# Changing the order of the filler work, and joining small steps, in a two-group hybrid encoder layer

## The chip, the cores and the metric

The kernel runs on one core of a Trainium2 chip. The metric is device time in microseconds (us) of one execution. The engines are named as in the profile: PE (matrix multiplications, with its weight loads as PEld), DVE, ACT and POOL (elementwise work), and SP, whose queue issues nearly all DMAs.

## The reference

One layer is applied to a prompt of 512 tokens and a sample of 1024 tokens, 1024 features each. Four mixers work on parts of one input projection, and their outputs, gated, go through one output projection:

```python
h = rms_norm(x, pre_g) * (1 + scale[:, None, :]) + shift[:, None, :]
proj = h @ w_in
a_q, a_k, a_v, a_lr, b_u, c_q, c_k, c_v, d_u, d_v, z = jnp.split(proj, splits, axis=-1)
out_a = gla_branch(a_q, a_k, a_v, a_lr, ...)      # chunked gated linear attention, both directions
out_b = fnet_branch(b_u, fnet_w)                  # Fourier transform over tokens and channels
out_c = attention_branch(c_q, c_k, c_v, ...)      # 8 query heads, 2 key heads, rms norm and rotary (rope)
out_d = sgu_branch(d_u, d_v, ...)                 # gating: w_s mixes 128 tokens, times d_u
mixed = jnp.concatenate([out_a, out_b, out_c, out_d], axis=-1) * jax.nn.silu(z)
y = rms_norm(mixed @ w_out, post_g)
return x + gate[:, None, :] * y
```

`scale`, `shift` and `gate` come from `silu(c) @ ada_w + ada_b`, one vector for the prompt and one for the sample.

## The kernel before

Everything is float32. Each operand of a large product is split in a high and a low part, and a product is made of three matmuls (high by high, high by low, low by high). The tokens are three groups of 512: group 2 is the prompt, groups 0 and 1 are the halves of the sample.

There are two streams of work. The **foreground** is a chain: GLA's first pass of a group (`gla_in`, six `level` steps, states), GLA's second pass (`gla_pass2`), FNet, the layout of keys and values (`kv_path`), and attention (`attend`). The **filler** is the projections, written under `later()`, which gives them a lower priority: `a_start` and `a_path` (GLA's q, k, v and low-rank gate), `zpath` (ten jobs, each evacuated by ACT and by one DVE product `zr`), `sgu` (two projections and the mixing product, tiles `dvu` and `vhl`), `b_path` (FNet's input), `c_kv` and `c_q` (keys and queries, with rope: tiles `kev`, `cev`, `rp_t`, `ropess`), and `out_ops`, `out_first`, `out_last` (the operand of the output projection, built per block of 128 features from a tile `mt` of the mixers' output and a tile `zt`, and the projection's column groups, `j` = 0 to 3). Small tables in DRAM (`zT`, `mixd`, `qd`, `kvd` and the like) carry results from filler to foreground and back.

The next group's operand is prepared in three steps: `in_prep_x(g)` loads the rows of x (`xt`), squares and sums them on ACT (`jk`, `xss`) and makes a scaled identity `rsb` on DVE; `in_prep_b` spreads it with one matmul of `ones` and `rsb`; `in_prep_t` loads x transposed (`xT`, stored under the tile `ze`), scales it on DVE (`h`, in the tile `zr`) and splits it into `oph` and `opl`. `gate_path` makes half of the output gate.

A scheduler at build time merges both streams into one fixed order per engine, by priority and modelled times; at run time each engine issues in that order, and an instruction that waits holds all behind it. A matmul level of GLA is tied to the filler: `LEVEL_AT` gives, per group, the thousands of filler columns after which the first level may be issued, and the step between levels. Filler products go to two PSUM buffers (`ps_mm`), scores and levels to three (`ps_s`), transposes to three, so a filler job can wait for the evacuation of the job before the last. Buffers in SBUF under one tag are shared: `xy` (two) by `xt`, `dvu`, `vhl` and `yt`; `ze` and `zr` (three each) by z, `xT`, `mt` and `zt`.

The filler's order is: group 2: a, z, sgu, b, then `queries(2, 0)`, which is in_prep_x(0), c_kv(2), in_prep_b, c_q(2) with in_prep_t(0), gate; group 0: a, z, sgu, b, then `queries(0, 1)`; group 1: b, a, z, sgu, c_kv. Beside the second pass and attention stand c_q(1), then the output projection of groups 2, 0 and 1. Sample attention has eight stages of eight score units; two pieces of filler (`fill_0`, `fill_1`) are written behind stages 3 and 5, since they need the attention output of group 0.

Of the kernel before, what the change touches and what calls it, by code (L numbers as in the profile page):

```python
# [36 lines left out]
HC = 3  # L37
# [3 lines left out]
LEVEL_AT = {2: (131, 12), 0: (571, 12), 1: (829, 12)}  # L41
# [3 lines left out]
def hybrid_encoder(  # L45
# [367 lines left out]
    def sgu(g):  # L413
# [91 lines left out]
    def c_q(g, hook):  # L505
# [375 lines left out]
    def gla_pass2(pool, gs, ap_all, u_f, u_b, pers):  # L881
        nb = 4 * len(gs)

        sf = pool.tile([128, nb, 64], F32, tag="sf", bufs=1, name="sf")
        sb = pool.tile([128, nb, 64], F32, tag="sb", bufs=1, name="sb")
# [522 lines left out]
```

## Time and profile before

| | |
|---|---|
| median of 3 runs | 1225.98 us (1222.92 to 1230.23) |
| the profiled execution | 1223.29 us, span 1221.5 us |
| PE busy | 1091.1 us, 89% of the span |
| DVE busy | 738.4 us, 60% |
| ACT busy | 597.8 us, 49% |
| POOL busy | 370.8 us, 30% |

The page shows the span in 40 slices of 30.5 us. A digit is the busy share of an engine in tenths, PEclk the clock that PE was granted, in tenths of full speed, and DMA the busy share of the DMA engines:

```profile
PE   5998899698999997889999997689999999979984
DVE  6437845769434257764237638956787666787505
ACT  4345455446454443353125344437675566656613
POOL 3136743654000044331104405563141003231003
PEclk9999899898999998989999998779999998989998
DMA  8498667966555574456878545466446324373272
```

Where PE shows less than 9, it waits, or the slice is at the ends of the program. In rows of single instructions further on, the first two numbers are start and duration in us, then engine, line, operation and tiles (out<-in), and in brackets the idle time just before it with what ended it. Rows of a group end with busy us, mean ns of one, and the idle time ahead.

### The profile page before, as it was taken

What the parts mean: (1) busy time and instruction counts of PE and PEld (TensorE: products, weight loads), DVE (VectorE), ACT (ScalarE), POOL (GpSimd) and SP (SyncE); (2) the same over time, 40 slices, a digit from 0 to 9 for tenths busy, and PEclk for the clock granted to TensorE, in tenths of its full rate; (3) what the DMA queues carried; (4) which work ended last, traced back from release to release, by engine and by line L of the source; (5) the groups of instructions that cost most, each with busy time, mean ns of one, the idle gap of its engine ahead of it and who ended that gap; (6) DMA issues with size and microseconds to landing.
All of it is one profiled execution on the core that took longest, in us unless ns stands there. A gap on an engine that the chain in (4) does not pass through costs nothing. (4 is left out here: it accounts for less than half of the span.)

```text
span 1221.5 us, 21183 instructions
## 1 busy us (share of the span) xinstructions
PE 1091.1 (89%) x7894; PEld 957.8 (78%) x7894; DVE 738.4 (60%) x1374; ACT 597.8 (49%) x1442; POOL 370.8 (30%) x327
## 2 busy tenths in 40 slices
PE   5998899698999997889999997689999999979984
PEld 1476689584988896757887896589989998969984
DVE  6437845769434257764237638956787666787505
ACT  4345455446454443353125344437675566656613
POOL 3136743654000044331104405563141003231003
PEclk9999899898999998989999998779999998989998
DMA  8498667966555574456878545466446324373272
GB/s 310 166 321 291 216 221 243 309 213 195 169 173 155 175 249 160 145 182 220 260 218 263 179 143 160 160 231 214 138 156 233 126 74 147 96 239 98 78 248 89
DMA packets 126391, 233.97 MB, mean 192 GB/s; under 512 B 13092, under 2 KB 65796, under 8 KB 126288
## 3 DMA queue, kind: packets, MB, share of 16 engines
q1 hardware_dynamic: 121624, 227.49, 57.3%
q10 hardware_dynamic: 4664, 5.13, 1.2%
q8 instruction: 62, 1.02, 0.3%
q14 instruction: 41, 0.34, 0.1%
HBM read 162.97 MB, written 69.61 MB: 190 GB/s over the span
## 5 line engine op out<-in xcount | busy, mean ns | idle before, releaser
L85 PE MATMUL ps_mm<-wt,oph 128*128 128x256 f32 x2240 | 440.1, 292 | 11.2 <-DMA wt<-parts 5.2
L85 PEld LDWEIGHTS ps_mm<-wt,oph 128*128 128x128 f32 x2240 | 364.0, 196 | 22.9 <-DMA wt<-parts 7.1
L85 PE MATMUL ps_mm<-wt,opl 128*128 128x256 f32 x1120 | 321.8, 289 | 0.0
L85 PEld LDWEIGHTS ps_mm<-wt,opl 128*128 128x128 f32 x1120 | 218.8, 196 | 1.5
L85 PE MATMUL ps_mm<-oph,wt 128*128 128x512 f32 x576 | 190.8, 401 | 14.8 <-DVE zr L100 6.7
L560 DVE TENSOR_REDUCE nm<-ps_s 128x1 f32<-128x512 f32 x160 | 109.0, 686 | 65.9 <-PE ps_s L559 65.0
L85 PEld LDWEIGHTS ps_mm<-oph,wt 128*128 128x128 f32 x576 | 108.2, 190 | 42.6 <-DVE zr L100 6.8
L97 DVE TENSOR_TENSOR ptl<-ps_t,pth 128x512 fp32r<-128x512 f32 x160 | 108.0, 684 | 42.3 <-ACT pth L577 41.9
L97 POOL TENSOR_TENSOR wt<-wr,wt 128x512 fp32r<-128x512 f32 (+1 forms) x68 | 89.3, 1317 | 129.9 <-ACT wt L307 124.7
L577 ACT CAST pth<-ps_t 128x512 fp32r<-128x512 f32 x160 | 91.2, 589 | 63.1 <-PE ps_t L575 62.0
L567 ACT ACTIVATE pr<-ps_s,nm 128x512 f32<-128x512 f32 x160 | 109.6, 691 | 24.2 <-DVE nm L563 19.0
L85 PE MATMUL ps_mm<-opl,wt 128*128 128x512 f32 x288 | 114.3, 397 | 0.0
L575 PE MATMUL ps_t<-cs,pr 128*128 128x128 f32 x640 | 93.5, 280 | 0.6 <-ACT pr L567 0.4
L100 POOL TENSOR_TENSOR oc<-oc,den 128x256 f32<-128x256 f32 x24 | 14.9, 629 | 242.2 <-DVE oc L103 207.2
L307 ACT CAST wt<-wr 128x512 fp32r<-128x512 f32 (+1 forms) x80 | 47.6, 598 | 83.1 <-PE ps_mm L85 56.0
L575 PEld LDWEIGHTS ps_t<-cs,pr 128*128 128x128 f32 x640 | 77.9, 145 | 11.1 <-ACT pr L567 2.2
L85 PEld LDWEIGHTS ps_mm<-opl,wt 128*128 128x128 f32 x288 | 54.9, 191 | 10.8
L558 PE MATMUL ps_s<-kT,qT 128*128 128x512 f32 x128 | 57.5, 449 | 6.2 <-ACT pr L567 6.1
L97 POOL TENSOR_TENSOR opl<-m,oph 128x512 fp32r<-128x512 f32 x30 | 40.2, 1350 | 67.3 <-ACT oph L1085 67.1
L559 PE MATMUL ps_s<-kT,qT 128*128 128x512 f32 x128 | 52.2, 408 | 0.0
L100 POOL TENSOR_TENSOR yt<-yt,gp 128x512 f32<-128x512 f32 x20 | 26.1, 1308 | 79.9 <-ACT jk L1117 79.8
L100 DVE TENSOR_TENSOR zr<-ps_mm,ze 128x512 f32<-128x512 f32 x30 | 20.7, 689 | 47.9 <-ACT ze L460 47.7
(332 smaller groups left out, 2087.9 us busy)
## 6 DMA issues: line engine op xcount, KB each, us to landing
wt<-parts SPq DMA_DIRECT2D x136, 512.0 KB, 3.8
parts<-wt SPq DMA_DIRECT2D x68, 512.0 KB, 4.3
wr<-wp SPq DMA_DIRECT2D x48, 256.0 KB, 3.0
adar<-ada SPq DMA_DIRECT2D x16, 512.0 KB, 6.7
zT<-zr SPq DMA_DIRECT2D x30, 256.0 KB, 2.1
zt<-zT SPq DMA_DIRECT2D x30, 256.0 KB, 4.2
mt<-mixd SPq DMA_DIRECT2D x24, 256.0 KB, 3.4
wr<-wo SPq DMA_DIRECT2D x20, 256.0 KB, 3.8
```

Of the source, the lines that this page charges most:

```text
L85: t = T.matmul(out, a, b, start=first and i == 0, stop=last and i == len(terms) - 1, skip_group_check=skip)
L97: e.tensor_tensor(out, a, b, ALU.subtract)
L100: e.tensor_tensor(out, a, b, ALU.mult)
L307: (V.tensor_copy if part_engine(HIGH_V, u, S) is V else S.copy)(h, raw)
L558: T.matmul(sp, qT[:, h, qc], kT[kv][:, kc], start=True, stop=False)
L559: T.matmul(sp, qT[:, h, qc], kT[2 + kv][:, kc], start=False, stop=True)
L560: V.tensor_reduce(nm[:, f:f + 1], sp, AX, ALU.max, negate=True)
L567: S.activation(pr, sps[f], AF.Exp, bias=nm[:, 0:1], accum_out=rsum[:, b, h, f:f + 1])
L575: T.transpose(pt[:, k * 128:(k + 1) * 128], pr[f][:, k * 128:(k + 1) * 128], ident)
L577: S.copy(pth[f][:, :, qc], ptv)
```

## The change

Four things change.

1. **The filler's order.** In_prep_x(0) moves from behind the mixing of group 2 to behind `a_start`, so its two loads of x are issued at the start of the program. c_kv(0), c_q(0) and in_prep_x(1) move ahead of z(0). In_prep_b, in_prep_t(1) and the gate for group 1 now stand with b(0) instead of with c_q(0). c_kv(1) and c_q(1) move ahead of z(1), and the gating of group 1 (`sgu`) takes c_q(1)'s place beside the second pass. `LEVEL_AT` has earlier columns.
2. **The output operand in parts.** `out_first` and `out_last` call a hook ahead of every column group `j`, and one or two blocks of the next operand are built at each.
3. **GLA's second pass.** The states of both directions stand in one tile `sfb`. Per block of 128 tokens there is one cast (`sh`) and one subtraction (`sl`) of 512 columns for both directions instead of two of 256, and the backward product `s` is made by POOL instead of DVE. The first and last block have one direction.
4. **The layout of keys.** `kv_path` casts and subtracts values in one step of 128x512 instead of four of 128x128, and keys in two of 128x512 instead of four of 128x256.

The diff, cut to its core:

```diff
@@ sgu, c_q, b_path
-    def sgu(g):
+    def sgu(g, hook=None):
...
         gemm_tm(opT[g], wp, JOFF[J_DV], 256, ev_v)
+        if hook:
+            hook()
         gemm_tm(opT[g], wp, JOFF[J_DU], 256, ev_u)
...
-    def c_q(g, hook):
+    def c_q(g, hook=lambda: None):
...
-    def b_path(g):
+    def b_path(g, hook=lambda: None):
         job[0] = ("b", g)
+        hook()
@@ kv_path
-        for b in range(4):
-            V.tensor_copy(vkv[:, kc + b, :, 0, :], kv[1][:, b])
-            sub(G, vkv[:, kc + b, :, 1, :], kv[1][:, b], vkv[:, kc + b, :, 0, :])
+        vh, vl = (vkv[:, kc:kc + 4, :, i, :] for i in range(2))
+        V.tensor_copy(vh, kv[1])
+        sub(G, vl, kv[1], vh)
...
-        for b in range(4):
-            S.copy(kst[:, b], kr[:, b].unsqueeze(2).to_broadcast([128, 2, 2, 64]))
-            sub(G, kl[:, b], kr[:, b].unsqueeze(2).to_broadcast([128, 2, 2, 64]), kst[:, b])
+        for i in range(2):
+            S.copy(kst[:, :, i], kr[:, :, i].unsqueeze(2).to_broadcast([128, 4, 2, 64]))
+            sub(G, kl[:, :, i], kr[:, :, i].unsqueeze(2).to_broadcast([128, 4, 2, 64]), kst[:, :, i])
@@ gla_pass2
-        sf = pool.tile([128, nb, 64], F32, tag="sf", bufs=1, name="sf")
-        sb = pool.tile([128, nb, 64], F32, tag="sb", bufs=1, name="sb")
+        sfb = pool.tile([128, 2, nb, 64], F32, tag="sfb", bufs=1, name="sfb")
+        sf, sb = sfb[:, 0], sfb[:, 1]
...
+                d0, d1 = (0 if j > 0 else 1), (2 if j < nb - 1 else 1)
+                s32 = pool.tile([128, 2, 4, 64], F32, tag="s32", bufs=2, name="s32")[:, d0:d1]
+                sh = pool.tile([128, 2, 4, 64], F32R, tag="sh", bufs=2, name="sh")[:, d0:d1]
+                sl = pool.tile([128, 2, 4, 64], F32R, tag="sl", bufs=2, name="sl")[:, d0:d1]
+                for d in range(d1 - d0):
+                    mul(G if d else V, s32[:, d], sfb[:, d0 + d, j, :].unsqueeze(1).to_broadcast([128, 4, 64]),
+                        hm.unsqueeze(2).to_broadcast([128, 4, 64]))
+                S.copy(sh, s32)
+                sub(V, sl, s32, sh)
                 terms = []
-                for d, (stt, on) in enumerate(((sf, j > 0), (sb, j < nb - 1))):
...
-                    mul(V, s32, stt[:, j, :].unsqueeze(1).to_broadcast([128, 4, 64]),
-                        hm.unsqueeze(2).to_broadcast([128, 4, 64]))
...
-                    S.copy(sh, s32)
-                    sub(V, sl, s32, sh)
@@ order of the jobs
-LEVEL_AT = {2: (131, 12), 0: (571, 12), 1: (829, 12)}
+LEVEL_AT = {2: (126, 12), 0: (546, 12), 1: (810, 12)}
...
-            jobs(2)
-            queries(2, 0)
-            jobs(0)
-            queries(0, 1)
-            jobs(1)
+            a_start()
+            rsb = in_prep_x(0)
+            zpath(2)
+            gating(2)
+            c_kv(2)
+            operand(0, rsb, lambda hook: c_q(2, hook))
+            a_path(0)
+            c_kv(0)
+            c_q(0)
+            rsb = in_prep_x(1)
+            zpath(0)
+            gating(0)
+            operand(1, rsb, lambda hook: b_path(0, hook))
+            b_path(1)
+            a_path(1)
             c_kv(1)
+            c_q(1)
+            zpath(1)
@@ new helpers
+    def gating(g, hook=None):
+        mix = sgu(g, hook)
+        next(mix)
+        if g == 2:
             b_path(g)
         next(mix, None)
...
+    def operand(n, rsb, job):
+
         in_prep_b(rsb)
-        c_q(g, lambda: in_prep_t(n, rsb, range(2)))
+        job(lambda: in_prep_t(n, rsb, range(2)))
         in_prep_t(n, rsb, range(2, KD))
         gate_path(n)
@@ output operand
-    def fill_0():
-        out_last(0, 6, ys0)
+    def some(g, tiles, at):
+
+        return lambda j: tiles.extend(out_ops(g, at.get(j, ())))
+
+    def fill_0():
+        out_last(0, 6, ys0, None, None, some(1, t1, {1: KORD[:2], 2: KORD[2:4], 3: KORD[4:6]}))
...
-        ys1.extend(out_first(1, out_ops(1, KORD[:8])))
+        t1.extend(out_ops(1, KORD[6:8]))
+        ys1.extend(out_first(1, t1))
...
-        c_q(1, lambda: t[0].extend(out_ops(2, KORD[:2])))
+        gating(1, lambda: t[0].extend(out_ops(2, KORD[:2])))
         t[0] += out_ops(2, KORD[2:6])
-        ys = out_first(2, t[0], lambda: t[1].extend(out_ops(2, KORD[6:])))
-        out_last(2, 6, ys, None, t[1], lambda: t[2].extend(out_ops(0, KORD[:6])))
+        ys = out_first(2, t[0], some(2, t[1], {1: KORD[6:7], 2: KORD[7:8], 3: KORD[8:]}))
+        out_last(2, 6, ys, None, t[1], some(0, t[2], {1: KORD[:2], 2: KORD[2:4], 3: KORD[4:6]}))
```

How this moves the work shows in the order of instructions of an engine. The first place is DVE, at GLA's levels for group 0 (`st` copies a level out of PSUM, `ql` and `k` prepare the next). Before:

```order
L127 TENSOR_SCALAR rs_v<-xss 128x4
L129 SCALAR_TENSOR_TENSOR rs_a<-rs_y 128x4
L100 TENSOR_TENSOR rs_b<-rs_a,rs_v 128x4
L133 SCALAR_TENSOR_TENSOR rs_r<-rs_b,rs_y 128x4
L207 TENSOR_SCALAR rsb<-cs,rs_r 128x128 x4
L829 COPY_PREDICATED st<-mk,ps_s 128x512 x3
L829 COPY_PREDICATED st<-mk,ps_o 128x512
L97 TENSOR_TENSOR ql<-q_6871,qh 128x2x16x16
L100 TENSOR_TENSOR k_6872<-k_6872,ng 128x2x16x16
L829 COPY_PREDICATED st<-mk,ps_s 128x512 x3
L829 COPY_PREDICATED st<-mk,ps_o 128x512
```

and now (line numbers are lower by one up to the second pass):

```order
L96 TENSOR_TENSOR ql<-q_6898,qh 128x2x8x32
L99 TENSOR_TENSOR k_6899<-k_6899,ng 128x2x8x32
L99 TENSOR_TENSOR zr<-ps_mm,ze 128x512
L830 COPY_PREDICATED st<-mk,ps_s 128x512 x3
L830 COPY_PREDICATED st<-mk,ps_o 128x512
L96 TENSOR_TENSOR ql<-q_6898,qh 128x2x4x64
L99 TENSOR_TENSOR k_6899<-k_6899,ng 128x2x4x64
L830 COPY_PREDICATED st<-mk,ps_s 128x512 x3
L830 COPY_PREDICATED st<-mk,ps_o 128x512
```

The steps of in_prep_x(1) (`rs_v` from `xss`, up to `rsb`) stood ahead of a level's copies; now evacuations of z(0) (`zr`) stand between the levels.

The second place is DVE in GLA's second pass, where both `s` products, `sl` and the transposed keys `kT` stand with the filler. Before:

```order
L100 TENSOR_TENSOR cev<-cev,rs_r 128x512
L133 SCALAR_TENSOR_TENSOR rs_r<-rs_b,rs_y 128x8
L100 TENSOR_TENSOR s_8768<-sb,cs 128x256
L100 TENSOR_TENSOR s_8788<-sb,cs 128x256
L100 TENSOR_TENSOR cev<-cev,rs_r 128x512
L487 COPY kT_8603<-ps_t 128x512
L487 COPY kT_8604<-ps_t 128x512
L487 COPY kT_8605<-ps_t 128x512
L487 COPY kT_8606<-ps_t 128x512
L100 TENSOR_TENSOR cev<-cev,rope_120 128x512
L103 TENSOR_TENSOR ap_all<-ps_o,ap_all 128x256
L97 TENSOR_TENSOR sl<-s_8768,sh 128x256
```

and now:

```order
L488 COPY kT_8631<-ps_t 128x512
L435 SCALAR_TENSOR_TENSOR dvu<-dvu,rs_r,sggt 128x256 x2
L99 TENSOR_TENSOR s_8763<-sfb,cs 128x256
L488 COPY kT_8632<-ps_t 128x512
L96 TENSOR_TENSOR wt<-wr,wt 128x512
L475 CAST vkv<-kvraw 128x8x64
L96 TENSOR_TENSOR sl<-s_8748,sh 128x512
L488 COPY kT_8633<-ps_t 128x512
L99 TENSOR_TENSOR s_8778<-sfb,cs 128x256
L488 COPY kT_8630<-ps_t 128x512
L488 COPY kT_8631<-ps_t 128x512
```

The rope steps of c_q(1) (`cev`, `rs_r`) are gone from it; the gating of group 1 (`dvu`) stands there. `sl` has 512 columns instead of 256, and every second `s` is gone from DVE.

The third place is SP's queue at the start of the program, where `adar` are the rows of the matrix behind scale and shift. Before:

```order
L368 DMA ongt<-ong 128x64
L168 DMA adar<-ada 128x1024
L368 DMA sggt<-sgg 128x256
L168 DMA adar<-ada 128x1024 x5
L276 DMA wr<-wp 128x512
```

and now:

```order
L367 DMA ongt<-ong 128x64
L167 DMA adar<-ada 128x1024
L367 DMA sggt<-sgg 128x256
L199 DMA xt<-x_s 128x2x1024 x2
L167 DMA adar<-ada 128x1024 x5
L275 DMA wr<-wp 128x512
```

The two loads of x for in_prep_x(0) stand ahead of `adar` loads that the start of the program uses.

More of the change, by code (lines that the diff above doesn't have):

```diff
@@ L913, in gla_pass2 @@
                 c = slice(b * 128, (b + 1) * 128)
-                terms = []
-                for d, (stt, on) in enumerate(((sf, j > 0), (sb, j < nb - 1))):
-                    if not on:
-                        continue
-                    s32 = pool.tile([128, 4, 64], F32, tag=f"s32{d}", bufs=2, name="s32")
-                    mul(V, s32, stt[:, j, :].unsqueeze(1).to_broadcast([128, 4, 64]),
-                        hm.unsqueeze(2).to_broadcast([128, 4, 64]))
-                    sh = pool.tile([128, 4, 64], F32R, tag=f"sh{d}", bufs=2, name="sh")
-                    sl = pool.tile([128, 4, 64], F32R, tag=f"sl{d}", bufs=2, name="sl")
-                    S.copy(sh, s32)
-                    sub(V, sl, s32, sh)
-                    qh, ql = hl[d]
-                    terms += [(qh[:, c], sh), (qh[:, c], sl), (ql[:, c], sh)]
+                d0, d1 = (0 if j > 0 else 1), (2 if j < nb - 1 else 1)
[7 more added lines that the diff above has]
+                sub(V, sl, s32, sh)
+                terms = []
+                for d in range(d1 - d0):
+                    qh, ql = hl[d0 + d]
+                    terms += [(qh[:, c], sh[:, d]), (qh[:, c], sl[:, d]), (ql[:, c], sh[:, d])]
                 o = ap_all[:, j, :]
@@ L1096, in ev @@
                 S.copy(ys[pair][:, :, j * 256:(j + 1) * 256], p.rearrange("p (b c) -> p b c", b=2))
-            if j == HC and hook:
-                hook()
+            if hook:
+                hook(j)
             gemm_tm(tiles, wo, j * KM * 256, 256, ev)
@@ L1147, in out_last @@
             for j in range(4):
-                if j == HC and hook:
-                    hook()
+                if hook:
+                    hook(j)
                 gemm_tm(tiles, wo, off[j], 256, evac(j))
@@ L1217, in hybrid_encoder @@
     ubd = [dram.tile([512, 256], F32, name=f"ubd{g}") for g in range(3)]
-    def jobs(g):
-        if g == 1:
-            b_path(g)
+    def gating(g, hook=None):
+        mix = sgu(g, hook)
+        next(mix)
         if g == 2:
-            a_start()
-        else:
-            a_path(g)
-        zpath(g)
-        mix = sgu(g)
-        next(mix)
-        if g != 1:
             b_path(g)
         next(mix, None)
-    def queries(g, n):
-        rsb = in_prep_x(n)
-        c_kv(g)
+    def operand(n, rsb, job):
         in_prep_b(rsb)
-        c_q(g, lambda: in_prep_t(n, rsb, range(2)))
+        job(lambda: in_prep_t(n, rsb, range(2)))
         in_prep_t(n, rsb, range(2, KD))
@@ L1288, in hybrid_encoder @@
     ys1 = []
+    t1 = []
+    def some(g, tiles, at):
+        return lambda j: tiles.extend(out_ops(g, at.get(j, ())))
     def fill_0():
[L1291 removed]
+        out_last(0, 6, ys0, None, None, some(1, t1, {1: KORD[:2], 2: KORD[2:4], 3: KORD[4:6]}))
     def fill_1():
[L1294 removed]
+        t1.extend(out_ops(1, KORD[6:8]))
+        ys1.extend(out_first(1, t1))
     with later():
         t = [[], [], []]
[L1298 removed]
+        gating(1, lambda: t[0].extend(out_ops(2, KORD[:2])))
         t[0] += out_ops(2, KORD[2:6])
[L1300 to L1301 removed]
+        ys = out_first(2, t[0], some(2, t[1], {1: KORD[6:7], 2: KORD[7:8], 3: KORD[8:]}))
+        out_last(2, 6, ys, None, t[1], some(0, t[2], {1: KORD[:2], 2: KORD[2:4], 3: KORD[4:6]}))
         ys0 = out_first(0, t[2])
```

1 line of the change is left out of this document (removed).

## The prediction

> **What bounds the kernel now.** The forty slices of the page come first: PE is at 9 in most of them and drops in a handful, and its granted clock drops in the same ones. The profiled execution took 1223.29 us (span 1221.5), 2.7 below the median of 1225.98; all sums below are made against 1223.29. PE issues in a fixed order and each wait holds everything behind it, so its idle time and its half-clock time are what a reordering can win; the change leaves its 7816 instructions as they are. Next I read windows by stage. Behind each stretch stand its length and the busy us of PE, PE's weight loads, DVE, ACT and POOL, then the granted PE clock, the DMA share and GB/s:
>
> ```profile
> 0.00:80.00 80.00, 66.26 (x278) 35.05 (x279) 41.95 (x73) 32.65 (x58) 23.20 (x22) 0.96 0.72 248
> 80.00:218.00 138.00, 125.40 (x976) 107.34 (x975) 85.26 (x130) 74.01 (x168) 74.48 (x54) 0.96 0.75 257
> 218.00:282.00 64.00, 48.11 (x335) 40.53 (x333) 47.04 (x101) 28.62 (x69) 38.45 (x40) 0.89 0.77 257
> 282.00:420.00 138.00, 135.94 (x786) 114.71 (x787) 66.73 (x113) 73.98 (x167) 12.66 (x15) 0.99 0.56 170
> 420.00:460.00 40.00, 38.28 (x310) 37.06 (x308) 19.25 (x33) 15.72 (x35) 15.14 (x11) 1.00 0.70 227
> 460.00:560.00 100.00, 80.68 (x737) 69.92 (x737) 69.71 (x136) 42.03 (x114) 32.07 (x27) 0.88 0.51 161
> 560.00:640.00 80.00, 76.39 (x457) 65.73 (x457) 25.07 (x67) 18.53 (x40) 11.11 (x13) 1.00 0.76 242
> 640.00:740.00 100.00, 97.12 (x867) 87.80 (x866) 58.88 (x112) 46.89 (x116) 32.18 (x24) 1.00 0.61 191
> 740.00:808.00 68.00, 44.55 (x273) 40.13 (x273) 63.72 (x118) 25.96 (x64) 42.11 (x38) 0.72 0.52 166
> 808.00:1162.00 354.00, 337.88 (x2572) 320.27 (x2571) 240.60 (x460) 224.41 (x567) 76.95 (x74) 0.97 0.47 151
> 1162.00:1221.00 59.00, 40.49 (x321) 39.25 (x320) 20.21 (x34) 14.97 (x49) 12.49 (x10) 0.87 0.50 174
> ```
>
> From each row I take idle time (length less PE busy) and an estimate of clock loss (PE busy times one less PEclk):
>
> - start, 0 to 80: 13.7 + 2.7
> - prompt GLA, 80 to 218: 12.6 + 5.0
> - prompt second pass, FNet, keys, 218 to 282: 15.9 + 5.3
> - prompt attention, 282 to 420: 2.1 + 1.4
> - group 0's GLA, 460 to 560: 19.3 + 9.7
> - group 1's GLA, 640 to 740: 2.9 + 0
> - keys and second pass, 740 to 808: 23.5 + 12.5
> - sample attention, 808 to 1162: 16.1 + 10.1
> - tail, from 1162: 18.5 + 5.3
>
> The two GLA stretches do the same work, yet group 0 loses 29 us in 100 and group 1 loses 2.9. Group 0 has rope and the preparation of the next operand beside it, group 1 z and gating jobs. Together with 740 to 808 (36 us in 68) these are the places the change rearranges.
>
> **Part A, group 0's GLA.** The waits, one instruction per row with the idle time before it and its releaser:
>
> ```profile
> 474.46 1.06 ACT L203 ACTIVATE jk<-xt 128x1024 bf16<-128x1024 f32 x1 [3.66 <-DMA xt<-x_s]
> 476.68 0.17 DVE L127 TENSOR_SCALAR rs_v<-xss 128x4 f32<-128x4 f32 x1 [5.94 <-ACT jk L203]
> 480.94 0.98 PE L824 MATMUL ps_s<-qh,kh 32*128 32x128 f32 x2 [5.67 <-DVE st L829]
> 512.09 0.75 DVE L252 SCALAR_TENSOR_TENSOR h<-xT,acol,rsb 128x512 f32<-128x512 f32 x1 [1.66 <-DMA xT<-xT]
> 520.73 0.48 PE L861 MATMUL ps_o<-vhl,sth 128*128 128x128 f32 x1 [7.04 <-ACT sth L856]
> ```
>
> ACT waits for the x rows of in_prep_x(1); DVE's `rs_v` of that sum waits 5.94 us for ACT; the masked copies `st` that empty the PSUM tiles of a GLA level stand behind it; PE waits 5.67. The second stall, 7.04, stands behind in_prep_t(1) (`h` waiting for the xT load) mixed with q rope. The change puts c_kv(0), c_q(0) and in_prep_x(1) ahead, so the levels run beside z(0), as group 1's do now. The first wait should go with its clock loss. The second may return: in_prep_b and in_prep_t(1) now stand beside b(0), where the last steps of group 0's GLA (`stl`, `ktl`) still are. Of 29 us I leave 12: 2.9 as in group 1's stretch, and one stall of 7.04 with some clock loss, 2 by estimate. So **−17**. Bounds: −23 (one small wait left), and −8 (only the first wait goes, with 2 us of clock).
>
> **Part B, the same wait in the prompt's second pass.**
>
> ```profile
> 236.16 1.19 PE L213 MATMUL ps_mm<-rsb,ones 128*128 128x512 f32 x1 [10.88 <-DVE rsb L207]
> ```
>
> In_prep_x(0) now has its x loads at the start of the program, so `rsb` is ready long before PE comes to it. The 10.88 goes, but PE then meets what stood behind it: fnet(2), keys, the wait for a weight tile. Of 10.9 and some 3 us at half clock I take **−9**; bounds 0 (the next wait ends just as late) and −14.
>
> **Part C, keys and second pass, 740 to 808.** One window inside it, then DVE's groups from 742 to 812 (busy us, mean ns):
>
> ```profile
> 780.00:800.00 20.00, 6.87 (x25) 4.49 (x23) 20.00 (x36) 7.75 (x19) 12.15 (x9) 0.57 0.42 144
> L100 DVE TENSOR_TENSOR cev<-cev,rs_r 128x512 f32<-128x512 f32 x4 | 5.5, 1377 | 0.0
> L103 DVE TENSOR_TENSOR cev<-cev,rp_t 128x512 f32<-128x512 f32 x4 | 4.8, 1196 | 0.0
> L100 DVE TENSOR_TENSOR cev<-cev,rope 128x512 f32<-128x512 f32 x4 | 4.6, 1138 | 0.0
> L400 DVE TENSOR_REDUCE ropess<-rp_t 128x8 f32<-128x512 f32 x4 | 2.7, 672 | 0.0
> L97 DVE TENSOR_TENSOR sl<-s,sh 128x256 fp32r<-128x256 f32 x14 | 7.5, 539 | 0.0
> L100 DVE TENSOR_TENSOR s<-sb,cs 128x256 f32<-128x256 f32 x7 | 5.0, 740 | 0.0
> L100 DVE TENSOR_TENSOR s<-sf,cs 128x256 f32<-128x256 f32 x7 | 2.9, 414 | 1.6 <-PE ps_o L85 1.6
> ```
>
> DVE is busy for all of 780 to 800 while PE does 6.87 at clock 0.57: here DVE ends last. The four rope groups of c_q(1) are 17.6 us of it (5.5 + 4.8 + 4.6 + 2.7), some 22 with the small rsqrt steps. They leave for group 1's GLA. In comes the gating of group 1, whose eight 128x256 steps on DVE go by this row (the norm steps have the same width):
>
> ```profile
> L447 DVE SCALAR_TENSOR_TENSOR dvu<-ps_mm,bst,dvu 128x256 f32<-128x256 f32 x12 | 5.2, 476 | 1.3 <-PE ps_mm L85 1.2
> ```
>
> That is 3.8 us. The joined steps: `sl`, 14 of 256 (7.5 us), becomes six of 512 and two of 256. By the row below for a subtraction of 512 (684 ns) and the 414 of the forward `s` for 256 that is 4.9, and saves 2.6. The seven backward `s` (5.0) go to POOL. The key layout's eight 128x128 casts become two of 512, saving about 2 by estimate.
>
> ```profile
> L97 DVE TENSOR_TENSOR ptl<-ps_t,pth 128x512 fp32r<-128x512 f32 x160 | 108.0, 684 | 42.3 <-ACT pth L577 41.9
> ```
>
> So DVE loses 22 + 2.6 + 5.0 + 2 and gains 3.8, about 28 of 68 us.
>
> At the same time more filler is offered: by the order of PE's instructions, the filler between the end of group 1's GLA and the first sample score grows by 49.7 thousand matmul columns. Four matmuls of 256 columns begin 0.46 us after the four before them:
>
> ```profile
> 1075.46 0.63 PE L85 MATMUL ps_o<-pth,vkv 128*128 128x256 f32 x4
> 1075.92 0.63 PE L85 MATMUL ps_o<-ptl,vkv 128*128 128x256 f32 x4
> ```
>
> so that is some 22 us of PE work, against 36 lost. It can only be used where the foreground waits. Half the loss filled seems fair: the chain of states, casts and additions remains serial, and the first `mt` loads, after which PE waits, still come from DRAM. **−19**; bounds −5 (only the joined steps show) and −28.
>
> Against the POOL step speaks this moment, the same 64-wide step on DVE alone and then beside POOL:
>
> ```profile
> 744.07 0.28 DVE L892 SCALAR_TENSOR_TENSOR sf<-sf,tfin,u_f 128x64 f32<-128x64 f32 x1
> 744.79 1.32 DVE L892 SCALAR_TENSOR_TENSOR sf<-sf,tfin,u_f 128x64 f32<-128x64 f32 x1
> 744.65 2.61 POOL L97 TENSOR_TENSOR iql<-q,iqh 128x512 fp32r<-128x512 f32 x2 [7.01 <-ACT iqh L908]
> ```
>
> 0.28 us alone, 1.32 while POOL subtracts: DVE was held for as long as POOL worked. The Trainium skill, "GPSIMD Engine Reference", section 8, says that GpSimd shares its SBUF interfaces with VectorE and contends with DVE instructions that have two SBUF inputs; the trace agrees here, 1.32 against 0.28. What a held DVE would do here is the first rival. "Perfetto Trace Analysis" of the Trainium skill, section "Optimizing Scalar/DVE Operations", says that where these engines aren't saturated but cause bubbles elsewhere, breaking instructions up may let work complete sooner; that speaks against joining. By it each of the eight blocks would come 0.27 us later (0.684 − 0.414), and the sum would be 2 us higher.
>
> **Part D, sample attention.** The output operand now comes in parts, one or two blocks ahead of each column group, instead of four to six at once. Rows on both sides of that:
>
> ```profile
> 1015.63 0.69 PE L1082 MATMUL ps_mm<-cs,mt 128*128 128x128 f32 x2 [2.90 <-DMA mt<-mixd]
> 1069.75 0.37 ACT L587 COPY ot<-ps_o 128x256 f32<-128x256 f32 x1 [0.95 <-PE ps_o L85]
> 1076.78 0.37 ACT L587 COPY ot<-ps_o 128x256 f32<-128x256 f32 x1
> 1103.12 0.37 ACT L587 COPY ot<-ps_o 128x256 f32<-128x256 f32 x1
> 1070.00:1078.00 8.00, 8.00 (x64) 7.42 (x62) 6.13 (x18) 7.02 (x22) 1.45 (x2) 1.00 0.61 187
> ```
>
> Three waits of about this size (2.90) stand in the stretch, 10 us with clock by estimate: **−6**, bounds 0 and −10. Its price is on the other side: filler used earlier is missing later. In PE's order, a run of about 15 score units (four score tiles each) and one of 5 have no filler, where before there were 7 and 2: 11 more. An `ot` copy ends two units. From 1069.75 to 1076.78 two units without much filler took 7.03 us, and the window row shows PE busy for all of it at full clock: loss 0. From 1076.78 to 1103.12 four took 26.34, or 6.1 more per pair, but there PE waited on an output block and on DVE too. Eleven units are 5.5 pairs: between 0 and +34. The first pair is the cleaner comparison, so I take 1.5 per pair, **+8**.
>
> **Part E, group 1's `gla_in`.** It takes in c_q(1)'s rope. The nearest case is the prompt's:
>
> ```profile
> 118.07 7.24 DVE L100 TENSOR_TENSOR ng<-ng 128x384 f32<-128x384 f32 x6
> 127.79 0.79 PE L85 MATMUL ps_mm<-oph,wt 128*128 128x512 f32 x1 [6.66 <-DVE zr L100]
> ```
>
> Six `ng` steps took 7.24 us beside POOL, `zr` came behind, and PE waited 6.66 for its PSUM tile. In group 1 now the same `ng` chain has rope between its steps and z(1) right behind. I take such a stall with a little clock, **+8**; bounds 0 (c_q's own evacuation is ACT's) and +14 (two).
>
> **Part F, the start.** Two 1 MB x loads now stand on SP's queue ahead of the last seven ada loads. DMA is busy 0.72 of 0 to 80, and PE already waits for ada there:
>
> ```profile
> 26.65 0.59 PE L160 MATMUL ps_t<-adal,sc 128*2 128x512 f32 x1 [4.26 <-DVE adal L97]
> ```
>
> 2 MB at the 248 GB/s of the first window row is 8 us, part of it in slack: **+3**, bounds 0 and +8. The earlier level positions and gla(2)'s other neighbours I put at 0, within 3 either way: its stalls (12.6) come from DVE's chain, which stays.
>
> **Sum.** −17 − 9 − 19 − 6 + 8 + 8 + 3 = −32: 1191 us.
>
> **The rivals.**
>
> *POOL holds DVE.* Rope and its POOL products move into `gla_in`(1), which has POOL work of its own, and seven more products go to POOL in the second pass. If DVE stays the engine that ends last there, C gives −5, E costs +12, D gives −3, with A −17, B −9, F +5, no-filler units +8: −9, or 1214. For it speaks the 1.32; against it that twenty-odd us of DVE work leave the stretch.
>
> *Attention starved, slower.* The filler doesn't fit the gaps of 740 to 808 and only delays the scores, then attention runs out of it. C −5, A −8, B −9, D 0, E and F 0, and the units without filler +34: +12, or 1235. It decides from about 2 us per missing unit, (8 + 9 + 5) / 11. For it: 26.34 us for four units. Against: 7.03 for two, PE full.
>
> *All of it is used.* C −28, A −23, the rest as in the forecast: −47, or 1176.
>
> That the change doesn't do what it says has no chance: the order shows the moves.
>
> **Chances.** Forecast 0.62 (its own range 1178 to 1208), POOL holds DVE 0.16, starved 0.14, all used 0.08. A measurement here tells 0.5%, about 6 us: faster is below 1219.8, slower above 1232.1. Forecast and "all used" are faster; of the first rival 0.10 faster and 0.06 the same; of the second 0.02 the same and 0.12 slower. Faster 0.80, same 0.08, slower 0.12. The range 1168 to 1222 leaves out the slower case and a little below.
>
> **What would show it.** A: idle plus clock loss of group 0's GLA at most 12 us, no PE wait behind `rs_v<-xss`. B: the product of `ones` and `rsb` without a wait. C: DVE no longer full for 20 us, PE over 0.8 busy between group 1's GLA and the first score. D: no PE wait over 2 us for `mt`, and the run of scores without filler near 3.5 us per unit; at 5.5 the second rival has won. E: one PE wait of 4 to 8 us on a z or c_q evacuation in `gla_in`(1). F: the first wait for `adal` no longer than 8 us. I am wrong if attention's length grows by more than the stretches ahead of it shrink.

## The result

The changed kernel took 1190.6 us (median of 4 runs, 1189.51 to 1196.34), against 1225.2 before (4 runs, 1222.92 to 1230.23): a ratio of 0.9722, 95% interval 0.9678 to 0.9765. The forecast was 1191. Its terms were less right than its sum, as the profile shows. The profiled execution took 1196.34 us (span 1194.5), so it is the slowest of the four. PE is busy 1085.3 us of it, 91% instead of 89%. The page counts 7894 matmuls on PE in both kernels, not 7816.

These are windows of the changed kernel. Their bounds follow the work: the end of the prompt's GLA states (206), the prompt's first and last scores (283, and 443 for group 0's first level), the end of group 0's GLA (516), of FNet (611), of group 1's GLA (743), the first and last sample scores (821, 1140). Columns are as in the prediction.

```profile
0.00:80.00 80.00, 64.38 (x267) 33.31 (x268) 40.56 (x73) 31.91 (x57) 24.67 (x22) 0.96 0.76 267
80.00:206.00 126.00, 117.41 (x902) 100.15 (x900) 76.17 (x118) 74.12 (x167) 68.99 (x49) 0.97 0.75 256
206.00:283.00 77.00, 65.56 (x433) 53.16 (x433) 70.68 (x118) 32.45 (x75) 52.02 (x45) 0.96 0.85 288
283.00:443.00 160.00, 153.98 (x1029) 138.06 (x1028) 98.72 (x188) 89.09 (x207) 36.78 (x37) 1.00 0.56 177
443.00:516.00 73.00, 71.90 (x719) 63.47 (x716) 44.48 (x80) 37.15 (x93) 17.57 (x12) 1.00 0.58 178
516.00:611.00 95.00, 86.48 (x545) 73.31 (x546) 21.95 (x69) 17.66 (x48) 12.75 (x14) 0.93 0.66 209
611.00:743.00 132.00, 117.86 (x895) 101.67 (x894) 75.19 (x137) 53.80 (x128) 41.43 (x31) 0.94 0.58 188
743.00:821.00 78.00, 68.04 (x534) 65.61 (x534) 59.03 (x90) 33.96 (x68) 52.62 (x39) 0.91 0.76 257
821.00:1140.00 319.00, 302.10 (x2298) 281.18 (x2298) 231.64 (x448) 209.53 (x543) 63.30 (x62) 0.99 0.41 133
1140.00:1194.00 54.00, 37.57 (x296) 36.52 (x294) 19.52 (x33) 14.10 (x47) 12.42 (x10) 0.89 0.51 181
```

Group 0's GLA (443 to 516) has PE busy 71.90 of 73 at full clock, where that GLA lost 28 us. Group 1's (611 to 743) has 117.86 of 132 at 0.94, and it lost 3 before. From 743 to 821 DVE is busy 59.03 of 78, and PE 68.04.

To compare kernels whose stages begin at different times, I summed PE's idle time and its clock loss (as in the prediction, busy time times one less PEclk) over windows of 2 us, between the same events of each kernel (first and last instruction of a stage on PE). The table holds what each stage lost in us, up to PE's last instruction, in one execution of each, for the two kernels and for five of the runs described below: e4 has the early x load taken back, e6 the late queries, e7 group 0's old order, e8 no rope for group 1's queries, and e9 the queries behind z. The sums differ by some us from what the spans would give, and PE's ends are modelled; a difference within 3 us is no finding.

| stage | before | changed | e4 | e6 | e7 | e8 | e9 |
|---|---|---|---|---|---|---|---|
| start, to 80 us | 16.3 | 18.4 | 15.8 | 18.5 | 17.9 | 19.0 | 16.8 |
| to the prompt's first level | 14.5 | 7.9 | 17.2 | 7.6 | 9.4 | 9.5 | 8.4 |
| prompt's GLA | 1.0 | 3.8 | 3.2 | 3.9 | 5.2 | 5.0 | 2.5 |
| prompt's second pass, FNet, keys | 20.1 | 14.7 | 25.8 | 14.8 | 14.8 | 17.4 | 16.1 |
| prompt's attention, to group 0's first level | 4.7 | 5.9 | 5.5 | 3.5 | 9.6 | 6.1 | 3.5 |
| group 0's GLA | 28.0 | 1.1 | 9.7 | 1.2 | 16.3 | 0.9 | 1.1 |
| FNet of the sample | 3.6 | 14.9 | 15.7 | 12.4 | 7.4 | 15.1 | 8.9 |
| to group 1's first level | 1.7 | 4.7 | 6.8 | 0.3 | 6.8 | 6.9 | 1.1 |
| group 1's GLA | 1.1 | 15.3 | 13.8 | 4.0 | 12.9 | 0.0 | 0.6 |
| keys and second pass | 34.4 | 14.2 | 14.3 | 37.4 | 21.9 | 13.9 | 13.4 |
| sample attention | 25.2 | 19.4 | 19.9 | 11.7 | 12.2 | 19.5 | 12.6 |
| tail | 8.6 | 7.3 | 5.8 | 7.6 | 5.5 | 5.8 | 5.7 |
| sum | 159.5 | 127.6 | 153.4 | 123.0 | 139.9 | 119.1 | 90.8 |

**Where it went wrong inside.** Single instructions of the changed kernel in group 1's GLA, of POOL, DVE and PE:

```profile
657.03 3.09 POOL L99 TENSOR_TENSOR rp_t<-cev,rope 128x256 f32<-128x256 f32 x2
655.99 2.16 DVE L99 TENSOR_TENSOR av<-av,own 128x1024 f32<-128x1024 f32 x1
659.32 1.88 DVE L102 TENSOR_TENSOR ap_all<-ap_all,av 128x1024 f32<-128x1024 f32 x1
627.81 1.22 DVE L99 TENSOR_TENSOR ap_all<-av,own 128x1024 f32<-128x1024 f32 x1
661.27 1.80 POOL L803 MEMSET st<- 128x2048 f32 x1 [1.14 <-DVE ap_all L102]
663.05 1.77 DVE L96 TENSOR_TENSOR ql<-q,qh 128x512 fp32r<-128x512 f32 x1
649.93 0.68 DVE L96 TENSOR_TENSOR ql<-q,qh 128x512 fp32r<-128x512 f32 x1
664.75 1.92 DVE L830 COPY_PREDICATED st<-mk,ps_s 128x512 f32<-128x512 uint8 x3
658.81 0.50 PE L84 MATMUL ps_mm<-oph,wt 128*128 128x512 f32 x1 [2.51 <-DVE zr L99]
665.61 1.58 PE L825 MATMUL ps_s<-qh,kh 32*128 32x128 f32 x3 [4.83 <-DVE st L830]
```

Rope's products hold POOL from 657.03 for 3.09 us, and DVE's steps beside POOL stretch: `av` takes 2.16 and `ap_all` 1.88, where a step of that width took 1.22 with POOL idle (627.81); `ql`, beside another POOL step, takes 1.77, where it took 0.68 with POOL idle (649.93). Four rope steps stand between them. POOL's clearing of `st` (661.27) waits for `ap_all`, since `av` lies in the same buffer, and the masked copies into `st` come at 664.75. PE waits 2.51 for `zr` and then 4.83 for `st`, at half clock from just behind the first. As in group 0's GLA in the kernel before, the masked copies stand behind filler work on DVE; there it was in_prep_x's, here it is rope's.

In the stretch of keys and second pass, one wait and two groups of DVE (743 to 821):

```profile
760.91 0.72 PE L487 MATMUL ps_t<-rc,kl 128*128 128x128 f32 x4 [4.08 <-DVE kT L488]
L99 DVE TENSOR_TENSOR s<-sfb,cs 128x256 f32<-128x256 f32 x8 | 7.3, 924 | 0.1
L901 DVE SCALAR_TENSOR_TENSOR sfb<-sfb,tfin,u_b 128x64 f32<-128x64 f32 x6 | 4.6, 759 | 0.1
```

Eight `s` products are left on DVE: seven forward, and the backward one of the first block, which has one direction. So six went to POOL, not the seven of the prediction. Those left take 924 ns each, against 414 for the forward ones before, and the 64-wide state steps 759 against some 280 undisturbed: DVE is still held there, yet PE loses 14 us instead of 34. The run e6 below shows that rope's absence is what makes the difference.

**Sample attention.** Twenty-microsecond windows of the run without filler, and two `ot` copies in it:

```profile
940.00:960.00 20.00, 17.35 (x126) 15.16 (x125) 15.04 (x32) 14.87 (x37) 2.57 (x2) 1.00 0.17 53
960.00:980.00 20.00, 17.77 (x130) 15.57 (x130) 16.18 (x36) 15.52 (x40) 2.65 (x4) 1.00 0.09 28
980.00:1000.00 20.00, 17.38 (x124) 14.72 (x124) 16.44 (x34) 16.84 (x44) 3.00 (x5) 1.00 0.24 72
948.52 0.37 ACT L588 COPY ot<-ps_o 128x256 f32<-128x256 f32 x1 [0.68 <-PE ps_o L84]
994.26 0.37 ACT L588 COPY ot<-ps_o 128x256 f32<-128x256 f32 x1
```

PE has no filler from 944.8 to 997.35. From 948.52 to 994.26 lie six pairs of units, 7.62 us each. PE is idle 2.65, 2.23 and 2.62 us in the three windows, 7.5 in all, at full clock, or about 1 us per pair. Attention isn't starved.

### The profile page after: what moved, and what is told of

The parts are those of the page before. It is cut to its first block, busy times and chain, and to the rows that moved or that the text cites. A ratio compares the mean times of both kernels' runs of the same rounds, so it can differ in the third digit from the quotient of the medians.

```text
span 1194.5 us, 21222 instructions
## 1 busy us (share of the span) xinstructions
PE 1085.3 (91%) x7894; PEld 946.4 (79%) x7894; DVE 737.9 (62%) x1349; ACT 593.8 (50%) x1428; POOL 382.6 (32%) x320
## 5 line engine op out<-in xcount | busy, mean ns | idle before, releaser
L84 PE MATMUL ps_mm<-oph,wt 128*128 128x512 f32 x576 | 192.8, 405 | 15.3 <-DMA wt<-parts 7.2
L96 POOL TENSOR_TENSOR wt<-wr,wt 128x512 fp32r<-128x512 f32 (+1 forms) x68 | 92.8, 1370 | 127.4 <-ACT wt L306 120.9
L576 PE MATMUL ps_t<-cs,pr 128*128 128x128 f32 x640 | 91.0, 275 | 4.0 <-DVE ptl L96 2.5
L576 PEld LDWEIGHTS ps_t<-cs,pr 128*128 128x128 f32 x640 | 75.1, 142 | 13.7 <-issue 2.0
L99 POOL TENSOR_TENSOR oc<-oc,den 128x256 f32<-128x256 f32 x24 | 14.9, 632 | 219.5 <-DVE oc L102 213.9
L84 PEld LDWEIGHTS ps_mm<-opl,wt 128*128 128x128 f32 x288 | 55.4, 193 | 11.4
L99 DVE TENSOR_TENSOR zr<-ps_mm,ze 128x512 f32<-128x512 f32 x30 | 20.6, 685 | 37.4 <-ACT ze L461 37.4
```

What stands on the lines that cost most here:

```text
L84: t = T.matmul(out, a, b, start=first and i == 0, stop=last and i == len(terms) - 1, skip_group_check=skip)
L96: e.tensor_tensor(out, a, b, ALU.subtract)
L99: e.tensor_tensor(out, a, b, ALU.mult)
L576: T.transpose(pt[:, k * 128:(k + 1) * 128], pr[f][:, k * 128:(k + 1) * 128], ident)
```

## The experiments

All of them are single edits of the changed kernel except e11, which edits the kernel before. Each was timed in three rounds with the kernel before on the same chip, and its ratio is to that; the changed kernel's is 0.9722 (0.9678 to 0.9765), and two kernels whose intervals overlap widely aren't told apart by their times.

**e7: group 0's filler as before.**

```diff
-            c_kv(0)
-            c_q(0)
-            rsb = in_prep_x(1)
             zpath(0)
-            gating(0)
-            operand(1, rsb, lambda hook: b_path(0, hook))
+            mix = sgu(0)
+            next(mix)
+            b_path(0)
+            next(mix, None)
+            rsb = in_prep_x(1)
+            c_kv(0)
+            operand(1, rsb, lambda hook: c_q(0, hook))
...
-LEVEL_AT = {2: (126, 12), 0: (546, 12), 1: (810, 12)}
+LEVEL_AT = {2: (126, 12), 0: (571, 12), 1: (810, 12)}
```

> The changed kernel with group 0's filler as before: z, gating, FNet's input, then in_prep_x(1), keys, queries with in_prep_t(1), and the later level columns of group 0. My theory: group 0's GLA loses some 28 us again where it now loses 1, and the stretch behind it loses 4 where it now loses 15: +16 us, 1207, with PE waits behind rs_v<-xss and in_prep_t. Rival: the stalls are of the same sum wherever this work stands: within 4 us of 1190.6.

Measured: 1208.12 us (1204.26 to 1212.54), ratio 0.9865 (0.9808 to 0.9923). So group 0's order is worth 17.5 us by the medians, near the 16 expected. The parts are not as expected, and the two profiled executions are only 9.8 us apart: group 0's GLA lost 16.3, not 28, FNet 7.4, and the stretch behind group 1's GLA 21.9. One wait stands out in group 0's GLA:

```profile
510.37 0.47 PE L862 MATMUL ps_o<-vhl,sth 128*128 128x128 f32 x1 [7.54 <-ACT sth L857]
```

It is the in_prep_t stall (7.04 before). The other one, behind `rs_v`, did not come back. Group 0's order is shown to matter by the time; how it splits over the two stalls is not.

**e6: group 1's queries beside the second pass again.**

```diff
-            c_kv(1)
-            c_q(1)
             zpath(1)
+            gating(1)
+            c_kv(1)
...
-        gating(1, lambda: t[0].extend(out_ops(2, KORD[:2])))
+        c_q(1, lambda: t[0].extend(out_ops(2, KORD[:2])))
...
-LEVEL_AT = {2: (126, 12), 0: (546, 12), 1: (810, 12)}
+LEVEL_AT = {2: (126, 12), 0: (546, 12), 1: (829, 12)}
```

> The changed kernel with the end of the filler as before: z, gating, keys of group 1, then its queries beside the second pass, and the later level columns of group 1. My theory: two terms trade. The 20 us won between group 1's GLA and the first score are lost again, the 17 us lost in group 1's GLA and just ahead of it come back: +3 us, 1194, with group 1's GLA losing under 4 us and the stretch behind it 30 or more. Rival, rope costs only in the second pass: +20, 1210. Rival, the move was a loss: under 1188.

Measured: 1189.61 us (1186.96 to 1193.92), ratio 0.9711 (0.9665 to 0.9757): no difference from the changed kernel. The table says why: 37.4 us are lost again in keys and second pass, and almost 16 of the 20 us come back in group 1's GLA and ahead of it, 8 more in attention. The waits of the second pass are those of the kernel before, the `mt` loads (5.77 and 2.91 there):

```profile
769.28 1.11 PE L1085 MATMUL ps_mm<-cs,mt 128*128 128x128 f32 x4 [7.53 <-DMA mt<-mixd]
773.24 1.11 PE L1085 MATMUL ps_mm<-cs,mt 128*128 128x128 f32 x4 [2.85 <-DMA mt<-mixd]
```

Moving the queries of group 1 to where the change has them, in exchange for the gating and with the earlier level columns, is worth nothing.

**e8: no rope for group 1's queries.**

```diff
-                rope(t.rearrange("p b (h d) -> p b h d", h=4), 2, 4, (4 if g == 1 else 0) + 2 * pair, 0, 1)
+                if g != 1:
+                    rope(t.rearrange("p b (h d) -> p b h d", h=4), 2, 4, (4 if g == 1 else 0) + 2 * pair, 0, 1)
```

> The changed kernel with the rotary step and norm of group 1's queries left out of the computation (the sample's second half attends with plain queries). It measures what this DVE and POOL work costs ahead of group 1's levels. My theory: the loss of group 1's GLA and of the stretch just ahead (15 and 5) falls to about 5 together, −13 us: 1178. Rival, the stalls there come from POOL's and DVE's own GLA steps: 1187 or more.

Measured: 1177.76 us (1176.90 to 1184.58), ratio 0.9622 (0.9579 to 0.9664), 12.8 less than the changed kernel. Group 1's GLA, from its first level to its last state, in a window of this run:

```profile
653.00:727.00 74.00, 74.00 (x621) 62.30 (x621) 33.62 (x60) 34.74 (x81) 14.79 (x10) 1.00 0.61 195
```

PE is busy for all 74 us at clock 1.00. The stall of the changed kernel there is rope's DVE and POOL work. The stretch just ahead kept its loss (6.9 against 4.7), so that part isn't rope's; PE waits for a weight tile there.

**e9 and e10: two other places for the same work.** In e9 the keys and queries of group 1 stand behind z(1), in e10 the queries stand ahead of the GLA projections.

```diff
             b_path(1)
             a_path(1)
-            c_kv(1)
-            c_q(1)
             zpath(1)
+            c_kv(1)
+            c_q(1)
```

> The changed kernel with group 1's keys and queries behind z(1) instead of ahead of it, the gating still beside the second pass. Rope then stands beside the last levels and the states of group 1's GLA, not in gla_in and not in the second pass. Theory that the loss of rope is that of the place (gla_in's chain of DVE steps, or the second pass's): the 17 us of group 1's GLA fall to some 8 and the second pass stays under 20, 1183. Rival, rope's DVE work costs wherever a GLA chain needs DVE: 1188 to 1194.

```diff
             b_path(1)
+            c_q(1)
             a_path(1)
             c_kv(1)
-            c_q(1)
             zpath(1)
...
-LEVEL_AT = {2: (126, 12), 0: (546, 12), 1: (810, 12)}
+LEVEL_AT = {2: (126, 12), 0: (546, 12), 1: (850, 12)}
```

> The changed kernel with group 1's queries ahead of its GLA projections, so that rope stands beside FNet, and the level columns of group 1 40 thousand later. Leaving rope out saved 13 us, which bounds the gain. Theory that DVE has room beside FNet: the 17 us of group 1's GLA fall to 5, 40 thousand columns (some 17 us of PE) are used earlier and cost 3 us more in attention without filler: 1182. Rival, FNet's chain meets the same DVE and POOL work: 1190 or more.

Measured: e9 1166.11 us (1157.84 to 1169.92), ratio 0.9518 (0.9468 to 0.9569); e10 1178.98 us (1176.52 to 1181.84), ratio 0.964. Both beat both kernels, and e9 is 24 us below the changed one. In e10 group 1's GLA lost 3.0 us, as its theory had it. Windows of e9 for FNet, group 1's GLA with what is ahead of it, keys and second pass, and attention:

```profile
513.00:607.00 94.00, 85.73 (x522) 72.61 (x523) 23.22 (x70) 20.97 (x47) 12.97 (x14) 1.00 0.72 231
607.00:709.00 102.00, 100.27 (x868) 89.82 (x867) 67.56 (x132) 51.17 (x127) 36.71 (x30) 1.00 0.64 205
709.00:787.00 78.00, 66.58 (x530) 64.03 (x529) 60.07 (x98) 33.54 (x68) 56.21 (x43) 0.96 0.76 260
787.00:1101.00 314.00, 303.10 (x2333) 284.77 (x2332) 230.71 (x444) 208.68 (x540) 62.23 (x61) 0.99 0.43 140
```

PE is busy 100.27 of 102 us in group 1's GLA (117.86 of 132 in the changed kernel), and keys and second pass lose no more than there. The rope work is all in e9, so it has a place where it costs almost nothing: behind the levels, beside the states and the start of the second pass. In these runs rope is dear where a chain of DVE steps is what PE waits for. That e9 gains more than leaving rope out (24 against 13) is not settled: by the profiles 7 us of it lie in attention (12.6 instead of 19.4, nearly all of it idle time) and 6 in FNet, where the changed kernel's profiled run lost 6.3 at half clock and e9's none (the last section shows what decides that). The profiled run of the changed kernel was its slowest, that of e9 its fastest, which makes the profiles differ by 38 us and the medians by 24.

**e4, e5 and e11: the early x load.** e4 puts in_prep_x(0) back, e5 only the prompt's level columns, e11 makes the early load the only change to the kernel before.

```diff
             a_start()
-            rsb = in_prep_x(0)
             zpath(2)
             gating(2)
+            rsb = in_prep_x(0)
             c_kv(2)
```

> The changed kernel with in_prep_x(0) behind the gating of the prompt, as before. My theory: the wait of PE for rsb (10.9 before) returns in the prompt's second pass, and the start wins 2 us back: +7, 1197, with the prompt's second pass, FNet and keys losing 22 instead of 15. Rival: with the joined steps the wait is hidden by what stands behind it: within 2 us of 1190.6.

```diff
-LEVEL_AT = {2: (126, 12), 0: (546, 12), 1: (810, 12)}
+LEVEL_AT = {2: (131, 12), 0: (546, 12), 1: (810, 12)}
```

> The changed kernel with the prompt's first level after 131 thousand columns as before, instead of 126. The loss ahead of that level fell from 14.5 to 8 in the changed kernel, which my prediction had at 0. Theory that the earlier level did it (the z job that waited 6.66 us behind the ng chain now stands behind the level's matmuls): +6, 1197, with that wait of 5 us or more back. Rival, it came from in_prep_x(0) or from chance: within 2 us of 1190.6.

```diff
         if g == 2:
             a_start()
+            first.append(in_prep_x(0))
...
-        rsb = in_prep_x(n)
+        rsb = rsb0 if n == 0 else in_prep_x(n)
```

> The kernel before with one part of the change alone: in_prep_x(0) right behind a_start. Taking this part out of the changed kernel cost 26 us, 9 of it ahead of the prompt's first level, 11 in its second pass, FNet and keys, 9 in group 0's GLA. Theory that it carries this by itself: the wait for rsb (10.9) and the 6.6 us wait behind the ng chain go, 1225 - 18 = 1207. Rival, taking it out only put the other moves in a wrong place (the level columns and the order fit the early load): the rsb wait alone goes, some 9, and 1216 is left.

Measured: e4 1216.32 us (1213.05 to 1221.55), ratio 0.9928 (0.9905 to 0.9951); e5 1194.85 (1190.88 to 1198.27), 0.9748; e11 1210.99 (1210.29 to 1214.61), 0.9900 (0.9868 to 0.9932), beside 1222.93 for the kernel before. So the early load is worth 12 us by itself, and taking it out of the changed kernel costs 26. PE's waits of e4:

```profile
128.40 0.79 PE L84 MATMUL ps_mm<-oph,wt 128*128 128x512 f32 x1 [6.57 <-DVE zr L99]
240.69 2.05 PE L212 MATMUL ps_mm<-rsb,ones 128*128 128x512 f32 x2 [11.73 <-DVE rs_a L128]
```

The second is the wait for `rsb` (10.88 before). The first is the one behind the `ng` chain (6.66 before). I had credited its end to the earlier level; e5 rejects that, since with the old columns the loss ahead of the first level stays at 7.7 and no wait of that size is there; its time, 4 us up, isn't told apart from the changed kernel's. e11 has it gone too (9.6), and the stage of `rsb` loses some 10 less there; its time lies between its theory and its rival, as 5 us come back in keys and second pass. The early load does it, though it has no instruction beside the `ng` chain: DVE's order there is different, one `zr` stands between the `ng` steps in the changed kernel, e5 and e11, and behind all six in e4 and in the kernel before. That the scheduler's modelled times, shifted by the early load, moved it is argued, not shown. Of the 26 us of e4, 9 lie ahead of the first level, 11 in the prompt's second pass, FNet and keys, and 9 in group 0's GLA; why that GLA loses more without the early load was not settled.

**e1 and e2: the joined steps.** e1 has `gla_pass2` and `kv_path` as before (the lines that the change replaced, not printed again), e2 only the backward product on DVE again:

```diff
-                    mul(G if d else V, s32[:, d], sfb[:, d0 + d, j, :].unsqueeze(1).to_broadcast([128, 4, 64]),
+                    mul(V, s32[:, d], sfb[:, d0 + d, j, :].unsqueeze(1).to_broadcast([128, 4, 64]),
```

> The changed kernel with the second pass and the key layout as they were before (steps of 256 and 128 columns, all s products on DVE). My theory: the joined steps take some 10 us off DVE between group 1's GLA and the first score (5.0 of backward products, 2.6 of subtractions, 2 of value casts), and about half of it was on the path: +4 us on the 1190.6 of the changed kernel, 1195, with the loss of PE (idle and half clock) in that stretch going from 14 to about 18. Rival, POOL holds DVE: the seven products on POOL cost DVE what they save, so 1188 to 1191.

> The changed kernel with the backward products of the second pass on DVE again, the steps still joined. Undoing all joined steps gave 1199, 8 us more, and the loss grew by 8 where the prompt's second pass, FNet and keys stand (15 to 22), by 2 behind group 1's GLA. Theory that the join of casts and subtractions carries that: 1190 to 1193. Theory that POOL's share carries it: 1196 to 1199. Rival, POOL holds DVE: under 1188.

Measured: e1 1199.27 us (1192.91 to 1204.59), ratio 0.9784 (0.9729 to 0.9839); e2 1195.84 (1194.59 to 1196.75), 0.9756 (0.9722 to 0.9790). Undoing all of it costs 8.7 us, POOL's share alone 5.2. Both intervals overlap the changed kernel's, so neither gain is certain, and how much of it is POOL's isn't either. "POOL holds DVE" would have made e2 faster; it isn't. The place is not the one I named: keys and second pass of the sample lost 15.7 and 16.1 against 14.2, the prompt's second pass, FNet and keys 22.2 and 20.4 against 14.7. That stage also lost 20.7 in e5, where the steps are joined, so its loss varies with the order by as much.

**e3: the operand's blocks at once.**

```diff
-            if hook:
-                hook(j)
+            if j == 3 and hook:
+                hook()
...
-        out_last(0, 6, ys0, None, None, some(1, t1, {1: KORD[:2], 2: KORD[2:4], 3: KORD[4:6]}))
+        out_last(0, 6, ys0)
...
```

> The changed kernel with the output operand's blocks built in one go ahead of the last column group, as before. My theory: PE's waits for mt in attention return (three or four of 2.5 to 3 us, some with half clock): +6 us, 1197. Rival: the filler's blocks are hidden by the score units of the foreground and attention gained from something else: within 2 us of 1190.6.

Measured: 1196.11 us (1189.93 to 1197.30), ratio 0.9750 (0.9703 to 0.9797). The sign and size are as expected, but the intervals overlap, and attention lost 18.7 us, no more than the changed kernel's 19.4; the rest was lost ahead of it, 21.9 in keys and second pass. There PE waits for `mt` just ahead of the first score:

```profile
806.95 1.09 PE L1085 MATMUL ps_mm<-cs,mt 128*128 128x128 f32 x4 [4.56 <-DMA mt<-mixd]
```

The parts are not shown to matter in attention.

## Why the prediction was right

Right in sum (−32 forecast, −34.6 by the medians, −27 between the two profiled runs), by the stages that it named first, with errors of both signs elsewhere, and with luck in how they met:

- **A, group 0's GLA, −17.** The GLA's loss fell by 27 us and FNet's behind it grew by 11, together −16 in the profiles; e7 puts it at 17.5. Right in size. But what came back is not what the prediction left standing: it kept in_prep_t's stall in the GLA, where only 1.1 us were lost. FNet's 11 lie at two waits for weight tiles, the first of them in `gate_path`, each with half clock behind it:

```profile
519.54 0.63 PE L159 MATMUL ps_mm<-wt,sc 128*2 128x512 f32 x2 [2.24 <-POOL wt L96]
550.60 0.69 PE L84 MATMUL ps_mm<-oph,wt 128*128 128x512 f32 x1 [2.19 <-DMA wt<-parts]
```

- **B, `rsb`, −9, and F, the start, +3.** The wait is gone, the stage lost 5 less, and the start 2 more. But the early load was worth 12 us alone and 26 in the changed kernel. The step that failed is the one that put gla(2)'s other neighbours at 0, as "its stalls (12.6) come from DVE's chain, which stays": the chain stayed, and the order of `zr` within it did not; the loss ahead of the first level fell by 7 us in the profile.
- **C, keys and second pass, −19.** −20.2 in the profile. Right in size. The split wasn't: taking rope away is nearly all of it (the stage loses 37.4 with it in e6, and 15.7 without the joins in e1).
- **D, sample attention, −6 and +8.** Measured −5.8 in all, where the two terms make +2. The price without filler came out near its 8, 7.5 us in the longer run, by more pairs at 1 us instead of 5.5 at 1.5. One wait for `mt` of 2.80 us remained, against the forecast of none over 2. What fell is not settled: e3 doesn't show it to be the operand's parts, and e6 and e9 with the same parts lose 7 us less still.
- **E, group 1's `gla_in`, +8.** That rope would cost there is right, as e8 shows; size and place aren't: +17 in the profile (14 in the GLA, 3 ahead, and those 3 aren't rope's), 12.8 by the time of e8. I had sized one stall on an evacuation, ahead of the levels, with a little clock; there were two, behind the start of the first level, the longer one at the masked copies, and the half clock lasted through both and beyond.

C and E are one move, forecast at −11, and e6 prices it at nothing: without it the time is 1 us less. B and F were forecast at −6, and the early load brought 12 alone and more with the rest. In the profiles E cost 9 more than forecast and B won 4 less, while D won 8 more and the stretch ahead of the prompt's first level 7 that were forecast at 0. To that extent it is luck that the sum came within 3 us; A is the term whose size an experiment bears out. Of the gain, group 0's order carries 17, the early load 12 alone, and the joined steps up to 9 that are not certain; they overlap, and don't add up exactly. Of the rivals, starved attention fell with the 7.62 us per pair. "POOL holds DVE" fell for the second pass, with C's −20 and with e2, which isn't faster; for group 1's GLA its 12 was nearer than the forecast's 8, and DVE is seen held there.

## What to carry to other kernels

When work of an engine must stand beside a chain, list the places it can stand and ask of each whether the chain's next step there needs the same engine. Here rope's DVE work in place of the gating cost 23 us in the second pass, some 13 to 15 around the first level, and almost nothing behind the last level, so a move between two bad places brought nothing and the third brought 24, not all of it rope's. And where a scheduler sets the order, an early load far away can change the order in a stage that it has no data in: read the order of that stage again after every move.

## What the runs showed of the hardware

I had counted clock loss for long waits only. In the changed kernel, short ones cost it too, but not all of them. Here are a wait of 1.79 us and one of 2.00, each with the windows of 3.41 us around it:

```profile
629.06 0.65 PE L84 MATMUL ps_mm<-wt,oph 128*128 128x256 f32 x2 [1.79 <-DMA wt<-parts]
625.84:629.25 3.41, 1.62 (x10) 1.01 (x9) 3.31 (x10) 2.27 (x5) 0.00 (x0) 1.00 0.93 313
629.25:632.66 3.41, 3.41 (x17) 3.41 (x17) 3.18 (x8) 2.17 (x5) 2.90 (x3) 0.50 0.03 5
632.66:636.08 3.42, 3.42 (x31) 3.42 (x30) 3.42 (x5) 1.76 (x4) 2.78 (x2) 1.00 0.40 108
650.66 0.33 PE L825 MATMUL ps_s<-ql,kh 32*128 32x128 f32 x3 [2.00 <-DVE ql L96]
646.32:649.73 3.41, 2.33 (x26) 1.71 (x25) 3.41 (x7) 0.94 (x2) 2.29 (x2) 1.00 0.45 113
649.73:653.14 3.41, 2.48 (x38) 2.19 (x39) 3.41 (x11) 0.72 (x3) 2.46 (x1) 1.00 0.34 123
```

After 1.79 us the granted clock is 0.50 for one window; after 2.00 us it stays at 1.00. PE's ends are modelled, but the pattern is wide: of the fourteen waits between 1.5 and 3 us of this execution that began at full clock, eight were followed by half clock (the shortest 1.54) and six were not (the longest 2.46).

What decides shows in when half clock begins. In the changed kernel's trace all its beginnings (120.66, 240.13 and 629.25 are three) lie whole multiples of 3.413 us apart, and the stretches within the program last 3.41, 6.83, 10.24 or 13.65 us. So the clock is set anew every 3.41 us, on a fixed grid, and it goes by how long PE was idle in the step that just ended. The wait of 1.79 lies within one step, which has PE busy for 1.62 of 3.41 us, and the next step runs at half clock. The wait of 2.00 is split at 649.73, and neither step has over 1.08 us idle. Of the steps at full clock (the clock's record begins at 11.4 us), all eight with 1.9 us idle or more were followed by half clock, four of eleven between 1.36 and 1.8, and none with less. In the thirteen profiled executions of this case together it was 95 of 95 with 1.9 us or more, and 4 of 2051 with less than 1.0.

The Trainium skill, "TensorE: Matmul & The Clock Gate", Part 1, gives one idle window of about 3.4 us as what throttles the clock, and adds that the window is free-running. The trace agrees on the length and the fixed grid; it differs on how idle a window must be, as 1.9 us of the 3.41 was always enough. Each such loss is one step or more at half speed, and which of the short waits pay depends on where they fall: the wait at FNet's weight tile had half clock in the changed kernel (2.19 us) and none in e9 (2.12 us), where a boundary of the grid split it into 1.38 and 0.74. A few us between two profiles can come from that alone.
